# One block of a feed-forward stage moved from the standard form to the seven-product form, with a longer run of products at the head

## The chip, the cores and the metric

The kernel runs on one core of a Trainium2 chip. The metric is the device time of one launch in microseconds (us). The engines are TensorE (PE; PEld is its weight load), VectorE (DVE), ScalarE (ACT), GpSimd (POOL) and SyncE (SP), which only issues transfers here.

## The reference

The reference is one inference step of a two-layer backbone on 640 tokens (128 of a prompt, 512 of a sample), with a model width of 1024. Each layer has two feed-forward stages, one before and one after a mixer, so there are four of them:

```
hn = modulate(rms_norm(x, g), shift, scale)
x  = x + 0.5 * gate * ((silu(hn @ w_gate) * (hn @ w_up)) @ w_down)
```

w_gate and w_up are 1024 x 2816 and w_down is 2816 x 1024, all float32. The mixers between the stages are not touched by the change.

## The kernel before

**Tokens and blocks.** The 640 tokens are two halves of 320, A and B. The 2816 columns of w_gate and w_up are 22 blocks of 128, numbered j. A float32 product is made of three matmuls: each operand is split into a rounded high part and the rest (wh and wl for weights, hi and lo for activations), and wh*hi, wh*lo and wl*hi are summed. For weights `w_split` does it: ScalarE copies the high part (L216) and VectorE subtracts for the rest (L217).

**A standard block** runs gate and up for A and B, 8 slices of 128 rows each, in `run_units` (L382 to L384): 2 * 2 * 8 * 3 = 96 matmuls of 128x320. It needs two `w_split` of 128x1024. `post` then does silu, a product (L668) and a split (L367) for each half of the tokens.

**A seven-product block** computes the same gate and up outputs by a scheme of the Strassen and Winograd kind: seven products P1 to P7, each over 4 row slices, so 7 * 4 * 3 = 84 matmuls (L745), on sums of weights and sums of activations. P1 and P2 take activations as they are (`hn.t`, quads) and weights as they are. P6, P5 and P7 take the sums f11, f12 and f22, P4 takes f21, and P3 takes plain activations with summed weights. The sums of activations are made once for each stage, on VectorE: `full` (L693) four times, L705, L706, L707 and L717, and a split of each (`t_split`, L366 and L367). The weights of a block come in two steps:

- `sums_load` brings a raw tile g, splits it (x1, for P1 and P2), and brings a tile s31 by two transfers of SyncE (L228, L229) and one adding transfer of GpSimd (L230). s31 has 2 buffers in the phase's pool.
- `sums_split` brings a raw tile u1, splits s31 (x2, for P7 and P5), overwrites s31 with two sums (L241, L242), splits it again (x3, for P6 and P3), and splits u1 (x4, for P4). s31's buffer is free after x3, and g's after L242.

Raw tiles have 4 buffers (RB), which the rows of the modulation weights (wm) share; split weights have 9 (WB), two for each split.

**Order.** In a stage the first two blocks are standard ones (in the three later stages A of both is woven into the end of the stage before, by `boundary`), then one more standard block (block 2, since NSTD is 3), then the rest as seven-product blocks, in groups that end at blocks 6, 11, 16 and 22. After each group comes a part of the down projection. The order on TensorE is the program's own (`manual_schedule`). `product_order` writes it for a group: first P1 and P2 of the blocks in `lead`, then the chains (P1, P6, P7, P4), (P5, P3) and (P2) of at most two blocks at a time, with at least three places between products of one chain. For the first group it gives, before the change:

```
P1(3) P2(3) P1(4) P2(4) | P6(3) P5(3) P6(4) P7(3) P3(3) P7(4) P4(3) P5(4)
P4(4) P1(5) P3(4) P5(5) P6(5) P2(5) P3(5) P7(5) P4(5)
```

The other engines' orders are a planner's: among the instructions that are ready, the one that stands earlier in the program, with the work after a product (L727, L751 and what follows) moved ahead by `TAP_EARLY`. `pump` puts rows of the modulation (L313, two VectorE instructions of 128x1024 each) behind the last weight split that the program has made.

Of the kernel before, what the change touches and what calls it, by code (L numbers as in the profile page):

```python
# [28 lines left out]
EPS = 1e-6  # L29
WB = 9  # L30
RB = 4
NSTD = 3
TAP_EARLY = 400
PE_TAPS = 16
RW = 655 + PE_TAPS - 4
# [36 lines left out]
def build(tc, ap):  # L72
# [3 lines left out]
    with ctx:  # L76
# [11 lines left out]
        def nm(p):  # L88
            uid[0] += 1
            return f"{p}_{uid[0]}"  # L90
# [71 lines left out]
        def add_unit(key, src, n, m):  # L162
            units[key] = (src, n, m)
            plan.append(key)

        for L in range(DEPTH):
            def ffn_units(f):
                for gi, (j0, j1) in enumerate(GROUPS):
                    for j in range(j0, j1):
                        if j < NSTD:  # L170
                            add_unit(("g", L, f, j), ap["wg"][L, f, j], 8, 128)
                            add_unit(("u", L, f, j), ap["wu"][L, f, j], 8, 128)
                        else:
                            add_unit(("s", L, f, j), ap["wgu"][L, f, j - NSTD], 8, 128)
                    for m in range(8):
# [25 lines left out]
        wpos = [0]  # L201
        LOOK = 2

        def raw_tile(src, n, m):
            raw = wpool.tile([P, n, m], F32, tag="raw", name=nm("wr"), bufs=RB)
            nc.sync.dma_start(out=raw, in_=src.rearrange("p (n m) -> p n m", m=m))
            return raw
# [4 lines left out]
        def w_split(src, n, m, **kw):  # L212
            pool = kw.pop("pool", wpool)
            hi = pool.tile([P, n, m], F32R, name=nm("wh"), **kw)
            lo = pool.tile([P, n, m], F32R, name=nm("wl"), **kw)
            S.copy(hi, src)  # L216
            state["paced"] = V.tensor_sub(lo, src, hi).ins  # L217
            return [hi[:, i, :] for i in range(n)], [lo[:, i, :] for i in range(n)]

        def half(x, i):  # L220
            return x[0][4 * i:4 * i + 4], x[1][4 * i:4 * i + 4]

        def sums_load(key):
            src, n, m = units[key]
            ph = state["pool"]
            s31 = ph.tile([P, 8, m], F32, tag="s31", name=nm("ws"), bufs=2)
            u0 = src[:, 0:4 * m].rearrange("p (n m) -> p n m", m=m)
            nc.sync.dma_start(out=s31[:, 0:4, :], in_=u0)  # L228
            nc.sync.dma_start(out=s31[:, 4:8, :], in_=u0)  # L229
            G.dma_start(out=s31, in_=src[:, 8 * m:16 * m].rearrange("p (n m) -> p n m", m=m), accum_op=ALU.add)  # L230
            g = raw_tile(src[:, 4 * m:12 * m], n, m)
            x1 = w_split(g, 8, m, tag="w", bufs=WB)
            loaded[key] = dict(P1=half(x1, 1), P2=half(x1, 0), s31=s31, g=g)

        def sums_split(key):
            src, n, m = units[key]
            ph, l = state["pool"], loaded[key]
            s31, g = l.pop("s31"), l.pop("g")
            u1 = raw_tile(src[:, 12 * m:16 * m], 4, m)
            x2 = w_split(s31, 8, m, tag="w", bufs=WB)  # L240
            V.tensor_add(s31[:, 0:4, :], g[:, 4:8, :], s31[:, 4:8, :])  # L241
            V.tensor_add(s31[:, 4:8, :], g[:, 0:4, :], s31[:, 0:4, :])  # L242
            x3 = w_split(s31, 8, m, tag="w", bufs=WB)
            x4 = w_split(u1, 4, m, tag="w2", bufs=4, pool=ph)
            l.update(P7=half(x2, 0), P5=half(x2, 1), P6=half(x3, 0), P3=half(x3, 1), P4=x4)
# [18 lines left out]
        index = {k: i for i, k in enumerate(plan)}  # L264
# [389 lines left out]
        def ffn(L, f, prev):  # L654
            isc, ish, ig = (1, 0, 2) if f == 0 else (7, 6, 8)
            keys = [[("g", L, f, j), ("u", L, f, j)] for j in range(NSTD)]
            rate_j, rate_m = RATES[L, f]
# [33 lines left out]
            def full(kh, H):  # L691
                t = ph.tile([P, 4, TH], F32, tag="h", name=nm("full"), bufs=6)
                V.tensor_add(t, hn.t[kh, H][0], hn.t[kh, H][1])  # L693
                return t

            def t_split(src, pool, tag, bufs):
                kw = dict(tag=tag, bufs=bufs) if bufs else dict(tag=tag)
                hi = pool.tile([P, 4, TH], F32R, name=nm("th"), **kw)
                lo = pool.tile([P, 4, TH], F32R, name=nm("tl"), **kw)
                split(src, hi, lo)  # L700
                return hi, lo

            sums_load(("s", L, f, NSTD))
            f12, f22, f11 = full(0, B), full(1, B), full(0, A)
            V.tensor_sub(f22, f22, f12)  # L705
            V.tensor_sub(f12, f11, f12)  # L706
# [4 lines left out]
            X["P7"] = t_split(f22, ph, "T", 6)  # L711
            for j in range(2, NSTD):
                for H in (A, B):
                    pg, pu = run_units(H, keys[j], hn)
                    post(H, j, pg, pu)
            f21 = full(1, A)
            V.scalar_tensor_tensor(out=f21, in0=f11, scalar=-1.0, in1=f21, op0=ALU.mult, op1=ALU.subtract)  # L717
            sums_load(("s", L, f, NSTD + 1))
            sums_split(("s", L, f, NSTD))
            X["P4"] = t_split(f21, spool, "s", None)  # L720
            sums_split(("s", L, f, NSTD + 1))
            wpos[0] = index["s", L, f, NSTD + 1] + 1
            state["sums"] = True

            def tap(src):
# [4 lines left out]
            def products(js, lead=()):  # L730
                bank, got, ended = {}, {}, set()
                for j, p in product_order(js, lead):
                    if p == "P1":
                        W(("s", L, f, j))
                    wh, wl = loaded["s", L, f, j][p]
                    xh, xl = X[p]
                    b = "a" if p in CHAIN[0] else "c" if p in CHAIN[1] else "b"
                    if (j, b) not in bank:
                        bank[j, b] = psum()
                    ps = bank[j, b]  # L740
                    first = p in ("P1", "P5", "P2")
                    final = p in ("P4", "P3", "P2")
                    for k in range(4):
                        for n, (l, r) in enumerate(((wh, xh), (wh, xl), (wl, xh))):
                            TE.matmul(ps[:, :TH], lhsT=l[k], rhs=r[:, k, :], start=(first and k == 0 and n == 0),  # L745
                                      stop=(k == 3 and n == 2), skip_group_check=True)
                    with tc.high_priority(offset=TAP_EARLY):
                        if p in ("P1", "P6", "P7", "P5"):
                            got[j, p] = tap(ps)
                        if p == "P2":  # L750
                            V.tensor_add(got[j, "P1"], ps[:, :TH], got[j, "P1"])  # L751
                            S.activation(out=got[j, "P1"], in_=got[j, "P1"], func=AF.Silu)
                        if p == "P3":
                            V.tensor_add(got[j, "P6"], ps[:, :TH], got[j, "P6"])
                            S.activation(out=got[j, "P6"], in_=got[j, "P6"], func=AF.Silu)
                        if (p == "P7" and (j, "P5") in got) or (p == "P5" and (j, "P7") in got):
                            V.tensor_add(got[j, "P7"], got[j, "P7"], got[j, "P5"])
                        ended.add((j, p))
                        if p in ("P4", "P3") and (j, "P4") in ended and (j, "P3") in ended:
                            hf = ph.tile([P, T], F32, tag="hf", name=nm("hf"), bufs=2)  # L760
                            V.scalar_tensor_tensor(out=hf[:, SL[A]], in0=bank[j, "a"][:, :TH], scalar=-1.0, in1=got[j, "P1"],
                                                   op0=ALU.mult, op1=ALU.mult)
                            V.scalar_tensor_tensor(out=hf[:, SL[B]], in0=got[j, "P7"], scalar=-1.0,
                                                   in1=got[j, "P6"], op0=ALU.mult, op1=ALU.mult)
                            h_tile(j)
                            split(hf, hts[j][:, 0, :], hts[j][:, 1, :])
                    if p == "P1":
                        pump(rate_j)

            for gi, (j0, j1) in enumerate(GROUPS):  # L770
                products(range(max(j0, NSTD), j1), (NSTD, NSTD + 1) if gi == 0 else ())
                if gi == len(GROUPS) - 1:
                    state["sums"] = False
                    for need in NEEDS[L, f]:
                        need_mod(L, need)
                if gi < len(GROUPS) - 1:
                    out_phase([("d", L, f, gi, m) for m in range(8)], [hts[j][:, 0, :] for j in range(j0, j1)],
                              [hts[j][:, 1, :] for j in range(j0, j1)], L, ig, False, rate=rate_m)
# [783 lines left out]
```

## Time and profile before

| what | value |
|---|---|
| median of 3 runs | 2657.86 us (2657.32 to 2660.58) |
| the profiled execution | 2652.47 us |
| its span, first to last instruction | 2650.7 us |
| TensorE busy | 2525.2 us (95%) |
| VectorE busy | 1936.4 us (73%) |
| ScalarE busy | 1245.7 us (47%) |

The span is what the rows below add up to; 1.8 us of the execution lie outside it. A busy share is a mean over the whole span, and the stages differ.

### The profile page before, as it was taken

The numbers are of one execution on the slowest core, as the hardware profiler recorded it, in microseconds if no ns is written. First come the engines' busy times: TensorE is split into PE (matmuls) and PEld (weight loads), VectorE is DVE, ScalarE is ACT, GpSimd is POOL, SyncE is SP. The second block draws the span as 40 slices with busy tenths as digits, with TensorE's granted clock in tenths as the row PEclk, the third lists the DMA queues.
The fourth block names the chain that finished last, engine by engine and source line by source line (L and its number), as shares of the span: only waits on it lengthen the run. The fifth ranks groups of instructions, "written<-read, shape, count | busy, mean of one in ns | idle before, by whom it ended". The sixth has DMA issues, their size and how long they took to land. (4 is left out here: it accounts for less than half of the span.)

```text
span 2650.7 us, 43732 instructions
## 1 busy us (share of the span) xinstructions
PE 2525.2 (95%) x17229; PEld 2434.1 (92%) x17229; DVE 1936.4 (73%) x3265; ACT 1245.7 (47%) x2316; POOL 154.4 (6%) x255
## 2 busy tenths in 40 slices
PE   7899999899999999999999999989999999999997
PEld 5899999889989999999999999989879998999997
DVE  6778878589986977677597777855985749554465
ACT  4444445458863644445354444543223536444552
POOL 0011110000000010101001011000000000101100
PEclk9999999999999999999999999999999999999999
DMA  7487876222112376767238687724431123656641
GB/s 283 122 225 205 214 220 168 76 70 64 48 53 88 104 207 182 204 187 196 80 116 212 182 227 210 198 93 123 133 112 64 56 72 112 175 143 147 157 120 58
DMA packets 140078, 378.09 MB, mean 143 GB/s; under 512 B 17504, under 2 KB 24160, under 8 KB 139360
## 3 DMA queue, kind: packets, MB, share of 16 engines
q1 hardware_dynamic: 111568, 296.33, 34.4%
q0 software_dynamic: 24768, 71.31, 15.2%
q10 hardware_dynamic: 3536, 7.66, 0.9%
q8 instruction: 135, 2.21, 0.3%
q14 instruction: 71, 0.58, 0.1%
HBM read 329.17 MB, written 3.67 MB: 126 GB/s over the span
## 5 line engine op out<-in xcount | busy, mean ns | idle before, releaser
L217 DVE TENSOR_TENSOR wl<-wr,wh 128x1024 fp32r<-128x1024 f32 (+3 forms) x393 | 390.6, 997 | 294.4 <-ACT wh L216 107.3
L216 ACT CAST wh<-wr 128x1024 fp32r<-128x1024 f32 (+3 forms) x393 | 339.7, 868 | 376.8 <-DMA wr<-in_wd 119.2
L384 PE MATMUL ps<-h,wl 128*128 128x320 f32 x1408 | 436.9, 310 | 9.8 <-DVE wl L217 9.8
L382 PE MATMUL ps<-h,wh 128*128 128x320 f32 x1408 | 437.0, 310 | 6.3 <-ACT h L366 6.3
L383 PE MATMUL ps<-h,wh 128*128 128x320 f32 x1408 | 436.1, 310 | 3.1 <-DVE h L367 3.1
L745 PE MATMUL ps<-quad,wh 128*128 128x320 f32 x1824 | 406.8, 311 | 3.8 <-ACT tmp L727 3.8
L745 PE MATMUL ps<-th,wh 128*128 128x320 f32 x1216 | 382.3, 314 | 28.4 <-ACT tmp L727 22.9
L745 PE MATMUL ps<-th,wl 128*128 128x320 f32 x1216 | 380.0, 313 | 3.6 <-DVE wl L217 3.6
L745 PE MATMUL ps<-tl,wh 128*128 128x320 f32 x1216 | 379.3, 312 | 0.0
L313 DVE CUSTOM_DVE_ANT_0 junk<-wm,crow,cv 128x1024 bf16<-128x1024 f32 x256 | 327.6, 1280 | 3.3 <-DMA wm<-in_wm 0.7
L382 PE MATMUL ps<-pair,wh 128*128 128x320 f32 (+1 forms) x976 | 309.3, 317 | 8.4 <-ACT pair L375 5.8
L745 PEld LDWEIGHTS ps<-quad,wh 128*128 128x128 f32 x1824 | 307.7, 189 | 4.6 <-ACT tmp L727 4.5
L383 PE MATMUL ps<-pair,wh 128*128 128x320 f32 (+1 forms) x976 | 304.0, 312 | 2.1 <-DVE pair L377 2.1
L384 PE MATMUL ps<-pair,wl 128*128 128x320 f32 (+1 forms) x976 | 303.7, 311 | 0.0
L745 PE MATMUL ps<-quad,wl 128*128 128x320 f32 x912 | 283.5, 311 | 4.9 <-DVE wl L217 4.9
L384 PEld LDWEIGHTS ps<-h,wl 128*128 128x128 f32 x1408 | 264.6, 188 | 14.0 <-DVE wl L217 14.0
L382 PEld LDWEIGHTS ps<-h,wh 128*128 128x128 f32 x1408 | 264.6, 188 | 8.3 <-ACT h L366 8.0
L383 PEld LDWEIGHTS ps<-h,wh 128*128 128x128 f32 x1408 | 264.6, 188 | 5.2 <-DVE h L367 4.7
L745 PEld LDWEIGHTS ps<-th,wh 128*128 128x128 f32 x1216 | 231.4, 190 | 35.4 <-ACT tmp L727 28.4
L217 DVE TENSOR_TENSOR wl<-ws,wh 128x1024 fp32r<-128x1024 f32 x152 | 185.3, 1222 | 92.0 <-ACT wh L216 37.0
L745 PEld LDWEIGHTS ps<-th,wl 128*128 128x128 f32 x1216 | 231.5, 190 | 4.9 <-DVE wl L217 4.9
L745 PEld LDWEIGHTS ps<-tl,wh 128*128 128x128 f32 x1216 | 231.5, 190 | 0.0
(262 smaller groups left out, 4398.1 us busy)
## 6 DMA issues: line engine op xcount, KB each, us to landing
wm<-in_wm SPq DMA_DIRECT2D x128, 512.0 KB, 4.4
wr<-in_wgu SPq DMA_DIRECT2D x76, 512.0 KB, 4.7
ws<-in_wgu SPq DMA_DIRECT2D x152, 256.0 KB, 3.9
ws<-in_wgu POOLq DMA_DIRECT2D x76, 512.0 KB, 6.8
x<-y POOLq DMA_DIRECT2D x96, 320.0 KB, 5.8
wr<-in_wd SPq DMA_DIRECT2D x64, 384.0 KB, 3.5
wr<-in_wd SPq DMA_DIRECT2D x64, 320.0 KB, 3.5
wr<-in_wgu SPq DMA_DIRECT2D x76, 256.0 KB, 3.8
```

Source lines behind the costliest of these rows:

```text
L216: S.copy(hi, src)
L217: state["paced"] = V.tensor_sub(lo, src, hi).ins
L313: V.tensor_tensor_reduce(out=junk[0], in0=w, in1=crow[cond], scale=1.0, scalar=cvc("b_mod", L * 72 + idx * KC + c), op0=ALU.mult, op1=ALU.add,
L382: TE.matmul(ps, lhsT=wh, rhs=xh, start=start, stop=False)
L383: TE.matmul(ps, lhsT=wh, rhs=xl, start=False, stop=False)
L384: TE.matmul(ps, lhsT=wl, rhs=xh, start=False, stop=stop)
L745: TE.matmul(ps[:, :TH], lhsT=l[k], rhs=r[:, k, :], start=(first and k == 0 and n == 0), stop=(k == 3 and n == 2), skip_group_check=True)
```

## The change

NSTD goes from 3 to 2, so block 2 of each of the four feed-forward stages becomes a seven-product block. The number of leading blocks becomes a constant LEAD of 3: P1 and P2 of blocks 2, 3 and 4 come first. `sums_load` of all three leading blocks stands ahead of the sums of activations in the program, where before the second one's stood behind them. In `sums_load` the raw tile g is asked for before s31. The order of the first group becomes

```
P1(2) P2(2) P1(3) P2(3) P1(4) P2(4) | P6(2) P5(2) P6(3) P7(2) P3(2) P7(3) P4(2) P5(3) P4(3) P6(4)
P3(3) P5(4) P7(4) P1(5) P3(4) P4(4) P6(5) P5(5) P2(5) P7(5) P3(5) P4(5)
```

```diff
@@ -29,7 +29,8 @@
-NSTD = 3
+NSTD = 2
+LEAD = 3
@@ -223,12 +224,12 @@
         def sums_load(key):
             src, n, m = units[key]
             ph = state["pool"]
+            g = raw_tile(src[:, 4 * m:12 * m], n, m)
             s31 = ph.tile([P, 8, m], F32, tag="s31", name=nm("ws"), bufs=2)
             u0 = src[:, 0:4 * m].rearrange("p (n m) -> p n m", m=m)
             nc.sync.dma_start(out=s31[:, 0:4, :], in_=u0)
             nc.sync.dma_start(out=s31[:, 4:8, :], in_=u0)
             G.dma_start(out=s31, in_=src[:, 8 * m:16 * m].rearrange("p (n m) -> p n m", m=m), accum_op=ALU.add)
-            g = raw_tile(src[:, 4 * m:12 * m], n, m)
             x1 = w_split(g, 8, m, tag="w", bufs=WB)
@@ -700,7 +701,8 @@
-            sums_load(("s", L, f, NSTD))
+            for j in range(NSTD, NSTD + LEAD):
+                sums_load(("s", L, f, j))
             f12, f22, f11 = full(0, B), full(1, B), full(0, A)
@@ -715,11 +717,11 @@
             f21 = full(1, A)
             V.scalar_tensor_tensor(out=f21, in0=f11, scalar=-1.0, in1=f21, op0=ALU.mult, op1=ALU.subtract)
-            sums_load(("s", L, f, NSTD + 1))
             sums_split(("s", L, f, NSTD))
             X["P4"] = t_split(f21, spool, "s", None)
-            sums_split(("s", L, f, NSTD + 1))
-            wpos[0] = index["s", L, f, NSTD + 1] + 1
+            for j in range(NSTD + 1, NSTD + LEAD):
+                sums_split(("s", L, f, j))
+            wpos[0] = index["s", L, f, NSTD + LEAD - 1] + 1
@@ -768,7 +770,7 @@
-                products(range(max(j0, NSTD), j1), (NSTD, NSTD + 1) if gi == 0 else ())
+                products(range(max(j0, NSTD), j1), range(NSTD, NSTD + LEAD) if gi == 0 else ())
```

## Rows read from the trace of the kernel before

**Rows 1.** The page: its span, and TensorE's busy time, share and instructions.
```profile
span 2650.7 us, 43732 instructions
...
PE 2525.2 (95%) x17229; PEld 2434.1 (92%) x17229; DVE 1936.4 (73%) x3265; ACT 1245.7 (47%) x2316; POOL 154.4 (6%) x255
```
**Rows 2.** TensorE's waits, second stage, 880 to 963 us: total, times, longest.
```profile
PE ps L745 <- ACT wh L216: 0.9, 1, 0.9
PE ps L745 <- DVE wl L217: 0.7, 1, 0.7
PE ps L745 <- ACT tmp L727: 0.6, 1, 0.6
```
**Rows 3.** Second stage by stretch: length; PE, PEld, DVE, ACT, POOL busy; PEclk; DMA.
```profile
907.50:921.45 13.95, 13.95 (x97) 13.95 (x96) 13.93 (x14) 7.27 (x9) 0.00 (x0) 1.00 0.01 1
...
934.31:940.93 6.62, 6.62 (x34) 6.62 (x35) 1.65 (x3) 2.42 (x4) 0.00 (x0) 0.74 0.81 222
```
**Rows 4.** TensorE in time, second stage: start, length, instruction, count.
```profile
928.49 0.31 PE L745 MATMUL ps<-th,wh 128*128 128x320 f32 x1
...
931.87 0.31 PE L745 MATMUL ps<-th,wl 128*128 128x320 f32 x1
...
962.89 0.31 PE L382 MATMUL ps<-h,wh 128*128 128x320 f32 x1
```
**Rows 5.** VectorE in time at the second stage's head.
```profile
896.87 1.23 DVE L217 TENSOR_TENSOR wl<-wr,wh 128x1024 fp32r<-128x1024 f32 x1
...
915.99 1.22 DVE L217 TENSOR_TENSOR wl<-wr,wh 128x1024 fp32r<-128x1024 f32 x1
917.12 1.48 DVE L693 TENSOR_TENSOR full<-quad,quad 128x1280 f32<-128x1280 f32 x1
918.53 0.48 DVE L367 TENSOR_TENSOR h<-tmp,h 128x320 fp32r<-128x320 f32 x1
918.93 1.48 DVE L717 SCALAR_TENSOR_TENSOR full<-full,full 128x1280 f32<-128x1280 f32 x1
920.33 1.22 DVE L217 TENSOR_TENSOR wl<-ws,wh 128x1024 fp32r<-128x1024 f32 x1
...
922.12 0.69 DVE L241 TENSOR_TENSOR ws<-wr,ws 128x512 f32<-128x512 f32 x1
...
923.15 0.69 DVE L242 TENSOR_TENSOR ws<-wr,ws 128x512 f32<-128x512 f32 x1
...
924.35 1.48 DVE L367 TENSOR_TENSOR tl<-full,th 128x1280 fp32r<-128x1280 f32 x1
925.75 0.48 DVE L751 TENSOR_TENSOR tmp<-ps,tmp 128x320 f32<-128x320 f32 x1
926.15 2.35 DVE L217 TENSOR_TENSOR wl<-ws,wh 128x1024 fp32r<-128x1024 f32 x2
```
**Rows 6.** Block 5's s31 in the second stage: SyncE's issue.
```profile
927.39 0.33 SPq L228 DMA_DIRECT2D ws<-in_wgu  x1
```
**Rows 7.** The same s31: ScalarE's high parts of x2 and x3.
```profile
939.91 1.05 ACT L216 CAST wh<-ws 128x1024 fp32r<-128x1024 f32 x1
...
944.34 1.05 ACT L216 CAST wh<-ws 128x1024 fp32r<-128x1024 f32 x1 [0.84 <-DVE ws L242]
```
**Rows 8.** First stage: VectorE's splits of f12, f11 and f22.
```profile
81.33 4.32 DVE L367 TENSOR_TENSOR tl<-full,th 128x1280 fp32r<-128x1280 f32 x3
```
**Rows 9.** First stage: TensorE, block 2's first matmul and a wait.
```profile
67.86 0.31 PE L382 MATMUL ps<-quad,wh 128*128 128x320 f32 x1
...
90.84 0.64 PE L745 MATMUL ps<-quad,wl 128*128 128x320 f32 x1 [4.92 <-DVE wl L217]
...
136.85 0.31 PE L382 MATMUL ps<-h,wh 128*128 128x320 f32 x1
```
**Rows 10.** First stage: TensorE's waits for taps, 55 to 137 us.
```profile
PE ps L745 <- ACT tmp L727: 3.3, 2, 1.7
```
**Rows 11.** First stage: TensorE's clock after that wait.
```profile
90.80:97.60 6.80, 5.99 (x24) 5.46 (x24) 6.05 (x8) 2.94 (x5) 0.00 (x0) 0.68 0.29 105
```

## The prediction

> **What bounds the kernel now.** I read the page first. TensorE is busy for 2525.2 of 2650.7 us [rows 1], so a matmul that goes away should pay unless something else ends the waits at that place. So I went on to TensorE's waits, cut to the head of one feed-forward stage. In the second stage they are small: 0.9 and 0.7 us for split weights in the products behind the lead, and 0.6 us late in the group [rows 2]. The third and fourth stages show the same pattern.
>
> The table by stretches shows why there is no more. While TensorE works on block 2 it never waits, but in the same 13.95 us VectorE is busy for 13.93 [rows 3]. Two engines are full side by side there, and the standard block is the work under which VectorE makes the sums of activations and the split weights. So the change is to be costed as a race: when does TensorE come to P6 of the first seven-product block, and when has VectorE its weights ready?
>
> **TensorE's side.** 24 matmuls of two products start between 928.49 and 931.87 [rows 4], so 23 steps take 3.38 us: 0.147 us each, 1.76 for a product of 12, 14.1 for a standard block of 96. Each stage issues 96 - 84 = 12 matmuls less, 1.76 us; over four stages 48 less, 7.0 us. That is all that the change can take off TensorE's own work.
>
> Block 2 ends at 921.45 in the second stage [rows 3], so it began at 907.4. Before, P6 came at 928.49, 21.1 us later. Now only six products stand between: 6 * 1.76 = 10.6, so TensorE wants P6(2) at 918.0.
>
> **VectorE's side.** Before, the first x3 is the first of the two splits at 926.15 [rows 5] and ends at 927.4; SyncE's issue for block 5's s31, which takes over that buffer, follows at 927.39 [rows 6]. What changes ahead of it:
>
> - Four weight splits stand between 896.87 and 915.99 [rows 5]: block 2's gate and up, and x1 of blocks 3 and 4. Now three x1 are wanted, in the first three places. The last one goes: 917.12 - 915.99 = 1.13 us.
> - Block 2's `post`, two L668 and two L367, goes: 4 at 0.40 (918.93 - 918.53) [rows 5], 1.6 us.
> - The split of u1 (x4), between L242 and the split of f21, falls behind x3: three g and one wm now hold the four raw buffers, so u1 waits until L242 frees one. 924.35 - 923.15 covers two instructions of 128x512 [rows 5], so 0.6 us less.
> - Three L751, not one, come first, moved ahead as they are: 2 at 0.40 (926.15 - 925.75) [rows 5], 0.8 us more.
>
> 927.4 - 1.13 - 1.6 - 0.6 + 0.8 = 924.9. I leave the order of the rest as it is: the splits of f12 and f22, and f21's two instructions, stand ahead of x2 in the program. TensorE waits from 918.0 to 924.9, 6.9 us, where it never waited before.
>
> **What is late next.** An idle TensorE restarts with a lower clock. After the 4.92 us wait of the first stage [rows 9] the next 6.80 us had a granted clock of 0.68 on average [rows 11], a mix of 1.2 and 2.4 GHz: 0.32 * 6.8 = 2.2 us lost. I charge that once in each stage. It is the nearest row; the smaller waits of the second stage cost 0.26 * 6.62 = 1.7 [rows 3].
>
> s31 has two buffers and now three blocks that want one at once. Block 4's transfers start when x3(2) is done. Block 5's did so before: issue at 927.39 [rows 6], high part of x2 at 939.91, of x3 at 944.34 [rows 7], whose rest ends 1.05 + 1.22 later if it queues for nothing: 19.2 us. Behind SyncE's waiting issue stand the raw tiles and the down weights; nothing of those is wanted sooner. So x3(4) is there at 924.9 + 19.2 = 944.1. TensorE reaches P6(4) after nine products, at 924.9 + 2.2 + 15.9 = 943.0, and waits 1.1. Thirteen products follow, 22.9, and the late 0.6 [rows 2]: the group ends at 967.6. It ended at 962.89 [rows 4]. The stage loses 4.7 us, and three stages 14.1. The waits of 0.9 and 0.7 and the old loss of clock are inside the old end, so they are counted.
>
> First stage: block 2's first matmul is at 67.86 [rows 9], so the six lead products end at 78.4. VectorE's splits of f12, f11 and f22 end at 85.65 [rows 8]. Two of four `post` instructions less and three L751 more make 86.05; f21 2.8 (918.53 - 917.12, 920.33 - 918.93), x2 1.13, L241 and L242 1.2 [rows 5], x3 1.05 + 1.22 [rows 7, 5]: 93.5. The wait grows from 4.92 to 15 us, but what comes after it is nearer to the end. x3(4) at 93.5 + 19.2 = 112.7 is later than TensorE (93.5 + 2.2 + 15.9 = 111.6); 22.9 more and the late waits of 3.3 [rows 10] end the group at 138.9. It ended at 136.85 [rows 9]: 2.1 us lost.
>
> Costed at nothing: block 2's extra weight traffic, because the adding transfer and SyncE's loads run while the transfers are nearly idle (a share of 0.01 while block 2 ran [rows 3]); without that cover it is the term of s31 that grows. Asking for g before s31 changes an order that the planner sets by free buffers anyway: nothing, or part of the second rival. The further taps and splits of block 2 fall on ScalarE and VectorE after the wait, where VectorE is busy for 1.65 of 6.62 us [rows 3].
>
> The sum is 14.1 + 2.1 = 16.2 us more: 2652.5 + 16.2 = 2668.7 on the profiled execution's own time. The median of the runs shown is 5.4 above that execution, so 2674 us.
>
> **Bounds.** x3(2) is late by 6.9 us at most if the order stays, and by nothing at best (first rival). The clock costs 1.7 to 2.2. s31 costs 19.2, or some 3 more (second rival). A kernel of this length can be told from no change at about 0.2%, 5.3 us.
>
> **The rivals.**
>
> - *The order gives way (faster).* Five instructions of 1.4 us need not stand ahead of x3(2): the splits of f12 and f22, f21's two, and the split of f21. Were all behind it, x3(2) would be there at 924.9 - 7.0 = 917.9, just when the lead ends; that is the point that decides. x3(4) comes at 937.1, the group ends at 960.6, 2.3 earlier than before, and the first stage 4.9 earlier: 11.8 us in all, 2646. For it speaks that the planner fills holes with what is ready; against it, that VectorE has no holes there and these five are older in the program, except the last.
> - *SyncE's queue holds s31 back (slower still).* If block 3's u1 is queued ahead of s31(4), it waits for a raw buffer until L242 of block 3, and s31(4) with it: x2, L241, L242 after x3(2), 2.3 us and the high part, some 3 us in each stage. 2674 + 12 = 2686. Four raw buffers, all taken, speak for it.
> - *The two sides balance (no change).* If half of those five instructions move, x3(2) is there some 4 us sooner, and the four stages come out within a few us: 2658.
> - *Only TensorE's work counts (faster).* VectorE's later work is hidden and the 7.0 us come off: 2651. Against it, VectorE's 13.93 of 13.95 us [rows 3]. By the Trainium skill (Perfetto Trace Analysis, Identifying the Most-Contended Engine) the engine with the highest occupancy is to be relieved first, which here is TensorE with its 95% [rows 1]; that would make this rival the forecast. Its next section, Optimization Strategy, allows that the engine changes from one regime to the next, and at these heads the trace agrees with that.
>
> **How the numbers follow.** Forecast 47%, SyncE's queue 14%, balance 15%, the order 15%, TensorE's work alone 9%. Slower than by 0.2%: 0.61; within: 0.15; faster: 0.24. The predicted time is the forecast's, 2674. The range goes from 2645, which takes in the faster rivals down to their price, to 2690, s31's delay with the worse clock. The forecast's own range is 2664 to 2686.
>
> **What would show it.** In the profile after, TensorE waits some 7 us once in stages two to four, ahead of the first matmul that reads `th` (P6 of block 2), put down to L216 or L217, and some 15 us in the first stage; the granted clock drops behind it; a wait of about 1 us comes nine products later; 48 matmuls are gone. VectorE is full without a hole until that wait ends. The prediction is wrong if x3(2) is split ahead of f21's sums, or if VectorE stands idle there.

## The result, and the profile after

The kernel after took 2685.09 us at the median (2676.97 to 2693.72, four runs) against 2658.4 before (2657.32 to 2660.58): a ratio of 1.0102, 95% interval 1.0082 to 1.0123. It is slower by about 27 us; the forecast was 16.

TensorE has 17181 matmuls where it had 17229 [rows 1], so the 48 are gone as the diff says. It is nevertheless busy for longer. The profiled execution of after is the slowest of its four runs (2693.72 us), so a second profile, of a run of 2680.29 us with a span of 2678.5, is used for sizes further down. The first lines of after's page:

```profile
span 2691.9 us, 43670 instructions
...
PE 2533.7 (94%) x17181; PEld 2440.5 (91%) x17181; DVE 1955.7 (73%) x3289; ACT 1255.7 (47%) x2336; POOL 158.0 (6%) x259
```

**Ahead of P6(2).** Most line numbers after are one or two higher than before (the product L747 was L745, the split of weights L217 and L218 were L216 and L217). TensorE in time, second stage of after, answering to [rows 4]:

```profile
936.30 0.64 PE L747 MATMUL ps<-th,wh 128*128 128x320 f32 x1 [5.27 <-ACT wh L217]
...
937.85 0.63 PE L747 MATMUL ps<-th,wl 128*128 128x320 f32 x1 [0.65 <-DVE wl L218]
...
981.07 0.31 PE L383 MATMUL ps<-h,wh 128*128 128x320 f32 x1
```

The first product that reads a sum of activations waits 5.27 us, and 0.65 more for the low part. The same two waits, 5.27 and 0.65, stand in the third and fourth stages, and 12.65 and 0.65 in the first. The matmul durations of 0.64 instead of 0.31 show the lower clock. The table by stretches, answering to [rows 3], has the cause beside it:

```profile
920.31:931.03 10.72, 10.72 (x74) 10.46 (x72) 10.31 (x11) 6.07 (x9) 0.00 (x0) 1.00 0.01 2
931.03:936.30 5.27, 0.00 (x1) 0.00 (x0) 5.24 (x6) 2.82 (x4) 0.00 (x0) 0.98 0.02 3
936.30:947.00 10.70, 10.05 (x49) 9.65 (x50) 6.45 (x8) 3.83 (x6) 0.87 (x1) 0.69 0.66 173
```

The six leads take 10.72 us. Then TensorE stands still while VectorE goes on without a hole (5.24 of 5.27 us), and in the 10.7 us behind the wait the granted clock is 0.69 on average, a mix of 1.2 and 2.4 GHz. What VectorE did in the wait, in time:

```profile
929.42 1.49 DVE L694 TENSOR_TENSOR full<-quad,quad 128x1280 f32<-128x1280 f32 x1
...
932.36 1.48 DVE L719 SCALAR_TENSOR_TENSOR full<-full,full 128x1280 f32<-128x1280 f32 x1
...
935.17 1.49 DVE L368 TENSOR_TENSOR tl<-full,th 128x1280 fp32r<-128x1280 f32 x1
936.58 2.35 DVE L218 TENSOR_TENSOR wl<-ws,wh 128x1024 fp32r<-128x1024 f32 x2
```

f21's two sums and its split stand ahead of x3(2) (the first of the two splits in the last row), in the order that [rows 5] had. x3(2) ends at 937.8, 17.5 us after the standard block.

**The s31 of later blocks.** SyncE's issues of s31(4) and, behind it, of s31(5), answering to [rows 6]:

```profile
937.83 0.33 SPq L230 DMA_DIRECT2D ws<-in_wgu  x1
...
943.58 0.33 SPq L230 DMA_DIRECT2D ws<-in_wgu  x1
945.40 0.33 SPq L307 DMA_DIRECT2D wm<-in_wm  x1
945.78 0.42 SPq L231 DMA_DIRECT2D ws<-in_wgu  x1
```

ScalarE's high parts of x2(4) and x3(4), answering to [rows 7]:

```profile
947.99 1.05 ACT L217 CAST wh<-ws 128x1024 fp32r<-128x1024 f32 x1 [3.34 <-DMA ws<-in_wgu]
...
952.33 1.05 ACT L217 CAST wh<-ws 128x1024 fp32r<-128x1024 f32 x1
```

From the issue to the end of x3(4) it takes some 17 us. TensorE never waits for x3(4) itself. But ScalarE stood 3.34 us at the first cast, with copies that free product banks behind it, and later 2.46 us at the cast of a raw tile (958.27), again with a copy behind it: TensorE waits 0.5 and 1.2 us for these copies.

**A wait that was not forecast.** In the boundary to the second stage TensorE waits 5.05 us at 892.95, on `quad` from ScalarE (L376); before, the longest wait there was 0.8. ScalarE in time in after (`crow` holds a row that the modulation is computed from; its Silu is L285):

```profile
882.71 0.82 ACTq L284 DMA_DIRECT2D crow<-in_cc  x2
...
886.12 0.39 ACT L376 ACTIVATE quad<-tmp,mod 128x128 fp32r<-128x128 f32 x1
...
891.49 1.06 ACT L285 ACTIVATE crow<-crow 128x1024 f32<-128x1024 f32 x1 [3.69 <-DMA crow<-in_cc]
892.46 0.73 ACT L376 ACTIVATE quad<-tmp,mod 128x192 fp32r<-128x192 f32 x2
```

and at the same place before:

```profile
878.70 1.42 ACT L375 ACTIVATE quad<-tmp,mod 128x128 fp32r<-128x128 f32 x4 [0.47 <-DVE tmp L373]
...
881.43 1.06 ACT L284 ACTIVATE crow<-crow 128x1024 f32<-128x1024 f32 x1
882.40 2.01 ACT L375 ACTIVATE quad<-tmp,mod 128x128 fp32r<-128x128 f32 x6
```

Two things differ. The Silu of crow now stands in ScalarE's order after one activation of hn, where five more stood ahead of it (the last four of them are the first row). And the data comes later: the view of transfers has, for the two crow loads in this boundary (KB each, median us to landing), after and then before:

```profile
crow<-in_cc ACTq DMA_DIRECT2D x2, 512.0 KB, 9.5
```

```profile
crow<-in_cc ACTq DMA_DIRECT2D x2, 512.0 KB, 6.7
```

The activations of hn stand behind the Silu in ScalarE's order and start when it has run (892.46), so they wait for a transfer that none of them needs.

**Where the time is.** This ledger is worked out from the starts of three matmuls in each stage, in TensorE's timeline: the first standard matmul of the stage, the first leading product and the first matmul of the down projection. In the second stage they are at 873.93, 921.45 and 962.89 before, and at 875.80, 912.28 and 973.05 in the second profile of after. "Boundary" is the change of the first interval with the 14.08 us of the missing standard block (96 matmuls) added back; "group" is the change of the second with 14.08 taken off (for three blocks neither). So boundary and group add up to what a head lost. "Elsewhere" is the rest of the span. All in us, one profiled execution each; the ratios are from all runs.

| kernel | ratio [95%] | group 1 | boundaries 2-4 | groups 2-4 | elsewhere | span |
|---|---|---|---|---|---|---|
| forecast | | 2.1 | 0 | 14.1 | 0 | +16.2 |
| after | 1.0102 [1.0082, 1.0123] | 4.0 | 8.2 | 21.0 | 8.0 | +41.3 |
| after_again | 1.0104 [1.0087, 1.0121] | 2.2 | 5.4 | 19.7 | 0.6 | +27.8 |
| order | 1.0072 [1.0046, 1.0098] | 7.1 | 5.1 | 15.4 | -5.8 | +21.8 |
| order4 | 1.0041 [1.0025, 1.0057] | 0.4 | 4.6 | 9.1 | 1.4 | +15.4 |
| gorder | 1.0082 [1.0058, 1.0106] | 3.3 | 6.3 | 22.8 | -2.8 | +29.6 |
| crowlate | 1.0072 [1.0050, 1.0093] | 1.3 | 3.9 | 22.2 | -5.9 | +21.6 |
| order4_crow | 1.0037 [1.0021, 1.0052] | 0.7 | 3.1 | 8.8 | 0.5 | +13.2 |
| order5_crow | 1.0052 [1.0035, 1.0069] | 3.5 | 2.8 | 8.5 | 1.5 | +16.3 |
| order4_crow_pool | 1.0036 [1.0022, 1.0050] | -5.4 | 12.9 | 8.4 | 1.0 | +16.8 |
| lead2 | 1.0157 [1.0136, 1.0178] | 4.0 | 14.6 | 26.4 | -6.6 | +38.4 |
| nstd3lead3 | 0.9997 [0.9982, 1.0012] | -6.6 | -1.0 | 1.6 | 23.9 | +17.8 |
| lessdve | 0.9988 [0.9973, 1.0003] | -2.9 | 5.0 | 1.1 | -3.5 | -0.2 |
| lessdve_crow | 0.9984 [0.9970, 0.9999] | -1.9 | 6.5 | -1.3 | 5.5 | +8.8 |

The column "elsewhere" differs from one execution to the next without any edit there (8.0 and 0.6 for the same kernel; the profiled run of nstd3lead3, at 2670.3 us, is the slowest of twelve whose median is 2652.0). So the heads are compared place by place, and whole times only by the ratios. In nstd3lead3 the clock is not the reason: its mean granted clock over the span is 0.987, as in the kernel before.

### The profile page after: what moved, and what is told of

It reads as the page before. It is cut to its first block, busy times and chain, and to the rows that moved or that the text cites. A ratio compares the mean times of both kernels' runs of the same rounds, so it can differ in the third digit from the quotient of the medians.

```text
span 2691.9 us, 43670 instructions
## 1 busy us (share of the span) xinstructions
PE 2533.7 (94%) x17181; PEld 2440.5 (91%) x17181; DVE 1955.7 (73%) x3289; ACT 1255.7 (47%) x2336; POOL 158.0 (6%) x259
## 5 line engine op out<-in xcount | busy, mean ns | idle before, releaser
L218 DVE TENSOR_TENSOR wl<-wr,wh 128x1024 fp32r<-128x1024 f32 (+3 forms) x393 | 388.6, 991 | 297.5 <-ACT wh L217 122.8
L217 ACT CAST wh<-wr 128x1024 fp32r<-128x1024 f32 (+3 forms) x393 | 338.5, 863 | 382.7 <-PE ps L385 106.6
L747 PE MATMUL ps<-th,wh 128*128 128x320 f32 x1280 | 407.1, 318 | 62.5 <-ACT tmp L729 31.4
L747 PE MATMUL ps<-quad,wh 128*128 128x320 f32 x1920 | 426.0, 310 | 2.1 <-ACT tmp L729 2.1
L747 PE MATMUL ps<-th,wl 128*128 128x320 f32 x1280 | 403.8, 315 | 5.8 <-DVE wl L218 5.8
L747 PE MATMUL ps<-tl,wh 128*128 128x320 f32 x1280 | 403.0, 315 | 0.0
L314 DVE CUSTOM_DVE_ANT_0 junk<-wm,crow,cv 128x1024 bf16<-128x1024 f32 x256 | 327.7, 1280 | 2.6
L747 PEld LDWEIGHTS ps<-quad,wh 128*128 128x128 f32 x1920 | 321.4, 188 | 2.9 <-ACT tmp L729 2.8
L747 PEld LDWEIGHTS ps<-th,wh 128*128 128x128 f32 x1280 | 247.2, 193 | 71.1 <-ACT tmp L729 38.1
L747 PE MATMUL ps<-quad,wl 128*128 128x320 f32 x960 | 297.0, 309 | 0.0
L218 DVE TENSOR_TENSOR wl<-ws,wh 128x1024 fp32r<-128x1024 f32 x160 | 195.1, 1221 | 107.1 <-ACT wh L217 57.7
L747 PEld LDWEIGHTS ps<-th,wl 128*128 128x128 f32 x1280 | 246.9, 193 | 8.5 <-DVE wl L218 8.5
L747 PEld LDWEIGHTS ps<-tl,wh 128*128 128x128 f32 x1280 | 247.2, 193 | 0.0
```

Of the source, the lines that this page charges most:

```text
L314: V.tensor_tensor_reduce(out=junk[0], in0=w, in1=crow[cond], scale=1.0, scalar=cvc("b_mod", L * 72 + idx * KC + c), op0=ALU.mult, op1=ALU.add,
```

## The experiments

The theory: VectorE's sums and splits lost the standard block that covered them. The rivals: the transfers of a third block (s31 has two buffers), the order in which they are asked for, and crow's rows, which come late at the boundary.

**order: x3(2) ahead in the program.**

```
             X["P6"] = t_split(f11, ph, "T", 6)
+            sums_split(("s", L, f, NSTD))
+            X["P5"] = t_split(f12, ph, "T", 6)
...
-            sums_split(("s", L, f, NSTD))
             X["P4"] = t_split(f21, spool, "s", None)
```

> The split of f11 comes first in the program, then the split weights of block 2, and only then the splits of f12 and f22 and f21's sums. VectorE's order as written out has the sums and split of f21 (three instructions, 4.2 us) behind x3(2), the splits of f12 and f22 still ahead. If VectorE's work as a whole is what is late (my theory), the wait ahead of P6(2) in stages 2 to 4 falls from 5.9 to some 1.7 us, but x3(3) has the same work ahead of it as in the kernel after and comes at about 942 where P6(3) is wanted 3.5 us after P6(2): a new wait of 4 to 5 us stands there, and the time stays within 5 us of the kernel after, 2680 to 2688. The rival of the prediction (the order gives way) saw only x3(2) and gains the 4.2 us and part of the clock in each stage: 2662 to 2668.

TensorE in time, second stage of order, at P6(2) and P6(3):

```profile
929.67 0.41 PE L747 MATMUL ps<-th,wl 128*128 128x320 f32 x1 [1.44 <-DVE wl L218]
...
937.72 0.63 PE L747 MATMUL ps<-th,wh 128*128 128x320 f32 x1 [4.55 <-ACT wh L217]
```

The wait moved, as my theory had it: 1.6 us at P6(2) (0.16 and 1.44) and 5.1 at P6(3) (4.55 and 0.56). In the first stage the wait of 12.7 became two of 6.3 and 6.2. The heads lost 27.6 us, as those of after_again with 27.3. The ratio is lower than after's, by intervals that overlap; in the profiled execution that came from elsewhere. The rival's 2662 to 2668 did not come, and my 2680 to 2688 was missed too: 2676.0.

**order4: f22's split and f21 held behind x3(3) as well.** `issue_after` sets what is made in it behind the instruction named; the first moves are those of order.

```
+            sums_split(("s", L, f, NSTD + 1))
+            with tc.issue_after(state["x3"]):
+                X["P7"] = t_split(f22, ph, "T", 6)
...
+            with tc.issue_after(state["x3"]):
+                f21 = full(1, A)
+                V.scalar_tensor_tensor(out=f21, in0=f11, scalar=-1.0, in1=f21, ...)
+                X["P4"] = t_split(f21, spool, "s", None)
```

> As in the run named order, and the split of f22, f21's sums and f21's split are held behind x3(3) on VectorE as well: 5.6 us of work less ahead of x3(2) and ahead of x3(3). Theory (cover lost, VectorE full): x3(2) comes at 932.2 instead of 937.8 in the second stage, where TensorE wants it at 931.0 to 931.7; x3(3) at 936.4 to 937.6, wanted at 935.7. So the waits of 5.9 us shrink to 1 to 3 in all, the first stage's 13.3 to some 8, and the slow clock behind them shrinks with them: 5 us per stage, 15 to 25 us in all, 2660 to 2670. If the loss comes from the transfers and the boundary instead, the waits move and the time stays above 2680.

The heads' loss fell from 27.3 to 14.0 us and the median to 2666.4, inside the forecast of the theory. The waits of the second stage's group (total, times, longest) are now short ones:

```profile
PE ps L751 <- DVE wl L218: 2.8, 3, 1.1
PE ps L751 <- DVE tl L369: 1.6, 1, 1.6
PE ps L751 <- ACT wh L217: 0.8, 2, 0.7
PE ps L751 <- ACT tmp L733: 0.6, 1, 0.6
```

and the clock behind them, in the table by stretches, does not fall (nor does it in the groups of the third and fourth stages):

```profile
924.20:934.90 10.70, 8.08 (x48) 7.04 (x49) 9.51 (x11) 4.25 (x8) 0.87 (x1) 1.00 0.58 142
934.90:941.00 6.10, 4.20 (x27) 3.67 (x26) 4.43 (x5) 3.65 (x6) 0.86 (x1) 1.00 0.56 185
```

**gorder: g asked for after s31, as before.**

```
-            g = raw_tile(src[:, 4 * m:12 * m], n, m)
             s31 = ph.tile([P, 8, m], F32, tag="s31", name=nm("ws"), bufs=2)
...
             G.dma_start(out=s31, in_=..., accum_op=ALU.add)
+            g = raw_tile(src[:, 4 * m:12 * m], n, m)
```

> Only the order of asking is undone: g after s31, as in the kernel before. Theory: the boundary's new waits (5.05 us in the second stage, 2.91 in the fourth) come from the sum of the transfers that are under way when the rows of crow are loaded, which stays; so they stay within 2 us and the time within 5 us of the kernel after, 2680 to 2690. Rival: the early g is what delays crow; then the boundary waits fall back to 0.8, and 6 to 8 us come off: 2677 to 2679. The wait ahead of P6(2) stays at 5 to 6 us in either case.

The boundary waits stay, 3.7 us in the second stage and 3.3 in the fourth, and so do the 5.3 us ahead of P6(2). The heads lost 32.3 us. The time, 2679.0 us, lies at the edge of both expectations and decides nothing; the waits do. Asking for g first is not what costs.

**crowlate: crow's loads and Silu written behind the leads' split weights.**

```
                 open_phase(1)
-                open_mod()
...
             state["sums"] = True
+            if prev is not None:
+                open_mod()
```

> The rows of crow are loaded and their Silu made after the split weights of the leads, in stages 2 to 4, instead of at the start of the phase. Theory (ScalarE stands blocked on crow's transfer with the activations of hn's second half behind it): the boundary waits of 5.05 and 2.91 us go back to 0.8 or less, 6 to 8 us come off: 2677 to 2679, and the wait ahead of P6(2) stays or grows by up to 1 us. Rival: these waits have another cause (VectorE or the transfers of the leads themselves): they stay, and the time with them, 2683 to 2688.

The edit did less than it says. The planner still issues both loads in the boundary, 0.2 and 3.1 us after its start, as in the kernel before; what moved is the Silu, which stands behind six activations of hn again. ScalarE in time:

```profile
872.62 0.36 ACTq L284 DMA_DIRECT2D crow<-in_cc  x1
...
877.18 1.42 ACT L376 ACTIVATE quad<-tmp,mod 128x128 fp32r<-128x128 f32 x4 [0.47 <-DVE tmp L374]
...
881.63 1.06 ACT L285 ACTIVATE crow<-crow 128x1024 f32<-128x1024 f32 x1 [1.73 <-DMA crow<-in_cc]
```

The first row lands 9.0 us after its issue, no sooner than in after (8.8), and the long wait is gone all the same: the second stage's boundary has no wait over 0.8 us, the fourth none over 0.8. So it is the Silu's place in ScalarE's order that makes the long wait, and not the later data alone. The time, 2674.9 us, is under the 2677 to 2679 of the theory. Yet the second boundary still lost 3.1 us. Its table by stretches shows why, and order4_crow (below), with waits of the same size at the same place, did not do this there. First crowlate, then order4_crow:

```profile
890.40:893.40 3.00, 2.12 (x9) 1.48 (x9) 3.00 (x8) 1.71 (x4) 0.00 (x0) 0.85 0.00 0
893.40:896.40 3.00, 2.96 (x10) 2.63 (x11) 3.00 (x7) 2.04 (x6) 0.00 (x0) 0.50 0.01 3
896.40:899.40 3.00, 3.00 (x12) 3.00 (x13) 2.73 (x5) 1.57 (x4) 0.00 (x0) 0.51 0.02 5
```

```profile
896.50:899.50 3.00, 2.12 (x13) 1.59 (x12) 3.00 (x8) 1.81 (x4) 0.00 (x0) 1.00 0.01 3
899.50:902.50 3.00, 2.19 (x13) 1.68 (x13) 3.00 (x8) 1.93 (x5) 0.00 (x0) 1.00 0.00 0
902.50:905.50 3.00, 3.00 (x22) 3.00 (x22) 3.00 (x4) 1.51 (x3) 0.00 (x0) 1.00 0.02 5
```

In crowlate the clock went to 1.2 GHz for some 6 us (10 and 12 matmuls in 3 us instead of 22), in order4_crow it stayed at 2.4. So the cause of the wait is shown, but what it is worth is not settled: the ratio is lower than after's by 0.003, with intervals that just overlap, and in the profiled run that is "elsewhere" and not in the heads.

**after_again: the kernel after as a yardstick.**

> The kernel after once more, unchanged, as the yardstick for the others of this call. Ratio to the kernel before 1.008 to 1.012, waits ahead of P6(2) of 5.3 us in stages 2 to 4 and 12.7 us in the first, boundary waits of 2 to 5 us. If its loss was an accident of the first runs, the ratio is under 1.005.

2680.29 us, ratio 1.0104, the same waits. The loss is no accident. Its clock behind the waits ahead of P6(2), first to fourth stage:

```profile
92.88:102.43 9.55, 8.91 (x38) 8.51 (x39) 6.44 (x8) 3.83 (x6) 0.86 (x1) 0.60 0.61 165
...
928.28:938.98 10.70, 9.65 (x49) 8.99 (x50) 6.44 (x8) 3.83 (x6) 0.87 (x1) 0.76 0.65 168
...
1389.87:1400.57 10.70, 10.05 (x45) 9.65 (x46) 6.44 (x8) 3.82 (x6) 0.88 (x1) 0.64 0.66 168
...
2261.16:2271.86 10.70, 10.06 (x48) 9.66 (x49) 6.44 (x8) 3.83 (x6) 0.86 (x1) 0.68 0.66 173
```

**order4_crow: both edits.** The diffs of order4 and crowlate together.

> Both edits that each took something back, order4 and crowlate, in one kernel. Theory (two separate losses, VectorE's late weights and crow's late transfer): they add, so 6 to 8 us come off the time of order4, which had a ratio of 1.0041 to the kernel before: 1.001 to 1.002, the boundary waits at 1 us or less each and the waits ahead of P6(2) and P6(3) as in order4. If the two were one loss that only shows in two places, the ratio stays at 1.004.

The boundary waits are gone as in crowlate and the groups are as in order4, but the ratio is 1.0037 where 1.001 to 1.002 was expected. The boundaries lose 3.1 us instead of order4's 4.6. So the two edits add in the profile, by 1.5 us and not by 6 to 8, and the ratio is the 1.004 of the other side of the expectation: beside order4, crow's wait is a small loss.

**lead2: four leads of two blocks.** The diff is `LEAD = 2`.

> Two standard blocks, but only four leading products of two blocks. Theory (the leads are the cover): 3.5 us of cover go, and with block 4's x1 and one sum behind a tap 1.5 us of VectorE's work go too, so the wait ahead of P6(2) grows from 5.9 by 2 us to 7.5 to 8.5 in stages 2 to 4. The third block's transfers are no longer asked for at the boundary, so the boundary waits fall to some 1 us, as with crowlate. In all within 8 us of the kernel after. Rival (the third block's transfers are what costs, by s31's two buffers): the wait does not grow and the time falls below 2670.

The table by stretches for its leads and the wait behind them:

```profile
916.02:923.10 7.08, 7.08 (x50) 6.94 (x48) 6.81 (x7) 5.08 (x7) 0.00 (x0) 1.00 0.00 0
923.10:932.60 9.50, 0.12 (x1) 0.00 (x0) 8.40 (x11) 2.81 (x5) 0.00 (x0) 0.73 0.16 55
```

With 3.6 us less cover the wait grew by 4.2 us, from 5.27 to 9.48: the leads are the cover, about one for one. VectorE's work did not shrink as I had said: the wait ends 16.7 us after the standard block, where in after it was 16.0, because a row of the modulation (L314, 1.28 us) and a hole of 1.03 us at ScalarE's high part stand there. The time, 2695.1 us, is 15 us over after_again, where I had said within 8. The boundary's part of my expectation fell too. With only two blocks asked for, the waits on `quad` are still 3.6 and 1.8 us, so it is not the third block that delays crow. The boundaries lost 14.6 us, at a granted clock of 0.87, 0.86 and 0.91 where after_again has 0.95, 0.91 and 0.90; why more was not tried.

**nstd3lead3: three standard blocks and six leads.** The diff against after is `NSTD = 3`.

> Three standard blocks as before, and six leading products of three blocks: the second half of the change alone. Theory: block 2 covers VectorE's work, so no wait over 2 us stands ahead of the first P6; the three blocks' transfers are still asked for at the boundary, so its waits stay at 2 to 5 us: 6 to 10 us over the kernel before, ratio 1.002 to 1.004. If the longer lead by itself is what costs (third g, third s31), the ratio is 1.008 or more; if the boundary's waits come from the missing block instead, it is 1.000.

The ratio is 0.9997, no change. No wait for split weights stands ahead of the first P6 in the second to fourth stages, and the longest boundary wait in the second is 0.8. That is the rival's 1.000: the boundary's wait comes with the missing standard block, not with the longer lead. The longer lead costs nothing by itself and takes 6.6 us off the first stage's group, whose waits sum to 7.8 us instead of 12.6.

**lessdve: VectorE's work taken out instead.**

```
-                split(src, hi, lo)
-                return hi, lo
+                S.copy(hi, src)
+                return hi, hi
...
-            f21 = full(1, A)
-            V.scalar_tensor_tensor(out=f21, ...)
-            X["P4"] = t_split(f21, spool, "s", None)
+            X["P4"] = X["P6"]
```

> The kernel after with less work for VectorE at the heads: the low parts of the four sums of activations are left out (the high part stands in their place) and so is f21 (P4 reads f11's parts). TensorE's matmuls, the weights and all transfers stay. That is 4 splits of 1.4 us and two sums of 1.4 us, 8.4 us less on VectorE in each stage, against a wait of 5.9 us ahead of P6(2). If VectorE's work without its cover is the cause, the waits ahead of P6(2) and P6(3) are under 1.5 us in stages 2 to 4 and 4 to 6 us in the first, the slow clock behind them goes, and the time is 2640 to 2655, under the kernel before: there TensorE's 7.0 us would show. If s31's transfers or the boundary are what costs, the waits come back a few products later and the time stays above 2665.

The second stage by stretches, the leads and what follows without a wait, and then the waits of that group:

```profile
906.89:917.45 10.56, 10.56 (x74) 10.56 (x73) 9.43 (x11) 8.04 (x12) 0.00 (x0) 1.00 0.09 29
917.45:924.00 6.55, 5.62 (x37) 5.10 (x36) 4.33 (x7) 3.22 (x6) 0.87 (x1) 1.00 0.72 187
```

```profile
PE ps L744 <- ACT tmp L726: 2.5, 2, 2.2
PE ps L744 <- DVE wl L218: 0.7, 1, 0.7
PE ps L744 <- ACT wh L217: 0.2, 1, 0.2
```

With the same number of matmuls and the same weights and transfers, the waits for split weights are down to 0.9 us and the clock behind the leads stays at 1.00. In the first stage they are still 8.7 and 1.7, more than expected. In all the heads lose 3.2 us instead of 27.3. The time, 2652.2 us, is inside the range; that it is under the kernel before is not established (0.9973 to 1.0003). VectorE's work is what ends the waits that make some 24 of the 27.3 us. The run takes 8.4 us of it away where the wait was 5.9, and one cast of 1.3 us on ScalarE goes too; that it is the missing cover that let this work show rests on lead2 and nstd3lead3.

**order5_crow: ScalarE's order mended too.** Against order4_crow, f22's and f21's casts stand behind the high part of x3(3), and block 4's casts behind f21's.

```
+            with tc.issue_after(state["x3"]), tc.issue_after(state["x3hi"]):
+                X["P7"] = t_split(f22, ph, "T", 6)
...
             for j in range(NSTD + 2, NSTD + LEAD):
+              with tc.issue_after(state["cast"]):
                 sums_split(("s", L, f, j))
```

> The kernel order4_crow with ScalarE's order mended in the same way: the casts of f22 and f21 stand behind the high part of x3(3), and the casts of block 4's s31, which waited for its transfer, behind the cast of f21. In order4_crow ScalarE made f22's cast ahead of x3(2) (1.3 us) and stood 4.7 us at s31(4) with f21's cast behind it, so that TensorE waited 1.1 and 1.6 us for them. Theory: these two go, 2 to 3 us in each stage, ratio 1.000 to 1.001. If ScalarE's order does not matter, the ratio stays at 1.003 to 1.004.

A miss: 1.0052. The second stage's group gained 2.4 us against order4_crow (its boundary and group in sum lost -0.3 instead of 2.2), but the first lost 2.8 and the third 1.4 more: split weights came late there under the new order (a wait of 2.0 us on L218 in the first stage, where order4_crow has none over 1.1).

**lessdve_crow: VectorE's work out and crow's Silu moved.** The diffs of lessdve and crowlate together.

> The kernel lessdve (the low parts of the four sums of activations and f21 are left out, the high parts and f11's parts stand in their places) with the rows of crow loaded behind the split weights of the leads as in crowlate. If VectorE's lost cover and crow's late transfer are the two losses and there is no third, the boundary's 5.0 us that lessdve still lost over the three boundaries shrink to under 2, and the time comes 3 to 5 us under that of lessdve: 2646 to 2650, ratio 0.996 to 0.998, TensorE's 7.0 us less work all but visible. If the boundary's loss is the clock that falls at any wait there, the ratio stays at 0.998 to 1.000.

2649.6 us, ratio 0.9984, at the edge of what was expected. The profiled run took 2661.3 us, and its boundaries lost 6.5 us though no wait there is longer than in the kernel before, so neither side of the expectation is borne out. By the interval at most 8 us are gained on the kernel before.

**order4_crow_pool: three sums on GpSimd.**

```
-            f12, f22, f11 = full(0, B), full(1, B), full(0, A)
+            f12, f22, f11 = full(0, B, G), full(1, B, G), full(0, A, G)
```

> The kernel order4_crow, with the three first sums of activations (f12, f22, f11; three instructions of 1.4 us on VectorE in each stage) made by GpSimd, which has no other work there but the issue of transfers. They are wanted some 25 us after their operands exist. If VectorE's amount of work still bounds the leads, 1 to 2 us come off each of stages 2 to 4 and up to 4 us off the first, whose wait of 6.4 us shrinks: 4 to 9 us in all, ratio 1.000 to 1.002. If GpSimd is slow enough that f11 comes late (more than some 8 us for one sum), or VectorE's instructions take longer beside it, the ratio is 1.004 or more.

The ratio is 1.0036, against 1.0037 without the edit, where 1.000 to 1.002 was expected. The first stage's group won 6 us, and the boundaries lost 10. GpSimd in time, and then VectorE beside it:

```profile
893.99 6.95 POOL L694 TENSOR_TENSOR full<-quad,quad 128x1280 f32<-128x1280 f32 x2 [0.98 <-DVE quad L379]
```

```profile
894.89 3.22 DVE L218 TENSOR_TENSOR wl<-wr,wh 128x1024 fp32r<-128x1024 f32 x1 [0.27 <-PE ps L385]
898.03 3.26 DVE L369 TENSOR_TENSOR h<-tmp,h 128x320 fp32r<-128x320 f32 x1
```

A sum takes 3.5 us on GpSimd (1.48 on VectorE), and one VectorE instruction beside each took 3.2 us where such ones take 1.22 and 0.48. So what VectorE was spared it lost standing. By the Trainium skill (SBUF — State Buffer, SBUF: two separate sides) the two engines share a pair of ports, and of a VectorE instruction with two inputs in SBUF and a GpSimd instruction that reads SBUF, the one that starts first holds the pair for its whole length and the other is blocked; these rows agree with that.

## Why the prediction was right in kind and short in size

**Right: the race and its two clocks.** TensorE wanted P6(2) 10.7 us after the standard block (forecast 10.6), and x3(2) was there after 17.5 (17.5). VectorE's order stayed as I had left it, and it was full until the wait ended. The idle time is 5.9 us and not 6.9, because the matmuls on the high part ran before the low part was there; 13.3 in the first stage, where 15 was forecast. The first stage's group lost 2.2 us in after_again, as forecast (2.1), but in part by luck: TensorE was idle for 17.0 us where the sum has 19.4 (15, 1.1 and 3.3), and busy for 54.2 where it has 51.6. That lost cover is the cause is shown from both sides: less cover (lead2) lengthens the wait, less VectorE work (lessdve) removes it, and a standard block more (nstd3lead3) covers it.

**Mis-sized: the clock.** I charged 2.2 us for a slow clock behind each wait, from one row. In after_again it cost (1 - 0.60) * 9.55 = 3.8, then 2.6, 3.9 and 3.4 us, 13.7 in all against 8.8, counted over these stretches alone.

**Mis-sized: the stage behind the wait.** I had x3(4) 1.1 us late at P6(4). s31(4) was quicker than its 19.2 us (17), and nothing waits for x3(4). What I left out is who stands behind a waiting cast in ScalarE's order: the copies of finished products. In the third stage of after_again x3(5) is late too, by 0.9 and 1.1 us; in the second stage of after, half of s31(5) was issued behind a tile of `wm` in SyncE's queue, which is the second rival's mechanism one block later. Over the three groups of after_again TensorE is idle for 25.6 us, and the sum has 25.8 (6.9, 1.1 and 0.6 in each): 2.9 less ahead of P6(2) and 2.8 more behind it, so that this agrees is luck. What makes the groups of stages two to four 19.7 us instead of 14.1 is that TensorE is busy for 160.6 us where the sum has 154.8, at a granted clock of 0.94, 0.92 and 0.94: over whole groups the clock cost some 12 us, and I had charged 6.6.

**Wrong: "costed at nothing".** I put the earlier transfers at nothing because they run while the transfers are idle. They are asked for at the boundary, and there crow's rows are loaded. The boundaries lost 5.4 us in after_again and 8.2 in after. That the place of crow's Silu in ScalarE's order makes the long wait is shown by crowlate, where the row came as late as in after. That it comes with the missing standard block, and not from the third one or from g's place, is shown by nstd3lead3, lead2 and gorder. Why the planner then put crow's Silu earlier, and what the 3 us are that the boundaries still lose in order4_crow, was not tried. What the wait is worth stays open, since the clock took back in crowlate what the wait had cost.

In us for after_again: 5.6 more in the groups, 5.4 in the boundaries and 0.6 elsewhere, on 16.2, are its 27.8.

**The rivals.** The price of "SyncE's queue holds s31 back", 2686, is nearest to the 2685.1 measured, but its mechanism did not come: s31(4) was issued at 937.83, when x3(2) was done. "The order gives way" had the wrong price. Its 2646 looked at x3(2) alone; order moved x3(2) ahead of three of the five instructions and found the wait again at P6(3), 3.5 us of products later. Only holding work behind x3(3) too (order4, four of the five) helped, and that is half of the loss. "Only TensorE's work counts" is what lessdve comes near: with VectorE out of the way some 3 us of the 7.0 show by the median, which is not clear of noise.

No version that does the whole work beats both kernels; nstd3lead3 is level with the kernel before. Two parts that won, six leads with three standard blocks in the first stage (6.6 us there) and GpSimd's sums in the first stage alone (6 us), were not run by themselves.

## What to carry to other kernels

Before shortening work on the busiest engine, look at which engine is full underneath it in that stretch: a block that goes away takes its cover along. Here 7.0 us of matmuls were saved and the heads still lost 27.3, so waits and slow clock took some 34. When a late operand is moved ahead in a full queue, cost the next operand as well; the queue's sum does not change. And an instruction that waits for a transfer is priced by what stands behind it on its engine: crow's Silu made a wait of 5.05 us for TensorE with five activations of hn behind it, and none over 0.8 behind these.

## What the runs showed of the hardware

- Short waits can leave TensorE's clock alone where one long wait does not: in order4, TensorE was busy for 8.08 of 10.70 us in pieces and the clock stayed at 1.00; in after_again one wait of 5.27 us was followed by 0.64 to 0.76 over the same length. Over the whole groups of stages two to four order4 has 1.00 with TensorE idle for 5.9, 8.3 and 6.2 us, and after_again 0.94, 0.92 and 0.94 with 8.0, 9.2 and 8.5 us.
- The same pattern of waits (none over 0.8 us) was followed by a clock of 0.50 for 6 us in one kernel's execution and by 1.00 in another's. The same kernel differs too: behind the second stage's wait of 5.27 us the clock was 0.69 in after and 0.76 in after_again. The Trainium skill (TensorE: Matmul & The Clock Gate, What's actually happening) says of a kernel's start that the number of slow matmuls differs from run to run; these rows show the like in the middle of one. It may be a part of what the column "elsewhere" shows, which was not tried.
- GpSimd's sum of 128x1280 took 3.5 us against 1.48 on VectorE, and the VectorE instruction beside it took 3.2 us.
